# Stores of the S5 tables on ScalarE and GpSimd, sums of squares in four column groups, another order of loads at the second FFN product

## The chip, the cores and the metric

The kernel runs on one core of a Trainium2 chip. Time is device time of one execution in microseconds; lower is better. The five engines have their own instruction streams and work in order: TensorE (PE), VectorE (DVE, `V` in the code), ScalarE (ACT, `S`), GpSimd (POOL, `G`) and SyncE (`SP`), which issues most DMAs. DMAs are issued from SP's, ACT's or POOL's stream and run beside the engines.

## The reference, cut

One inference step of a decoder trunk with two layers, on 1,024 prompt tokens and 64 sample tokens (NT = 1,088), width 1,024, in fp32. Layer 0 mixes tokens by retention and by dilated windowed attention, layer 1 by an S5 state-space model. Behind each mixer stands an FFN, and a norm stands ahead of each.

```python
def rms_norm(x, g):
    xf = x.astype(jnp.float32)
    y = xf * lax.rsqrt(jnp.mean(xf * xf, axis=-1, keepdims=True) + EPS)
    return (y * g.astype(jnp.float32)).astype(x.dtype)

def swiglu(h, w_in, w_out):
    gate, up = jnp.split(h @ w_in, 2, axis=-1)
    return (jax.nn.silu(gate) * up) @ w_out
...
# layer 0:  x += ab_mixer(rms_norm(x));  x += swiglu(rms_norm(x))
# layer 1:  x += s5_mixer(rms_norm(x));  x += swiglu(rms_norm(x));  y = rms_norm(x)
```

The S5 model has 64 groups of 16 channels with 64 complex states each. Its matrices per group (input, output, powers of the state matrix) follow from the weights alone, so they can be worked out at any time before layer 1.

## The kernel before

Activations lie with the features on the 128 partitions: x is eight tiles x[:, m] of 128 features by 1,088 tokens (1,092 with padding). Each fp32 operand is split into a rounded part (hi) and a rest (lo), and each product is three matmuls: hi by hi, and the two mixed ones. ACT writes the hi part, DVE (or POOL) the lo part: `wh_i`/`wl_i` for weights of the second product (`w_unit`, L810 and L811), `wh_p`/`wl_p` for those of the first (L1389, L1390), `f_hi`/`f_lo`, `a_hi`/`a_lo` and others for activations (`load_a`, L1590 and L1591).

`ffn` runs both FFNs. The **first product** (L1414) works on units of 256 columns, each made of seven products of 24 matmuls; weights of a product are split ahead of it, into four buffers. The results go through `put` into a tile `sg`, and from there to a DRAM tensor `a_d` in two stores (L1560). A store is kept in `pending` and issued during the next unit; the last one is `last_store`. The **second product** (`out_proj`, matmuls at L171) goes four times over the eight output tiles m, each time with a part of the 22 activation tiles f: 0 to 4, 5 to 10, 11 to 15, 16 to 21. In the first pass the m are taken in the order FIRST = 6, 7, 4, 5, 2, 3, 0, 1, later from 0 to 7. The result of one (f, m) is collected in one of two PSUM buffers `big` and added to x[:, m] by DVE (L1604), which frees the buffer. Between the products stands the **handover**: f_lo tiles 0 to 4 are loaded from a_d (L1587) and split, the last a_d store is issued, and x is loaded from `x_d` (L1620), each behind the one before (`behind` holds an instruction back until a given one has been placed).

Beside layer 0's FFN runs a background generator, `s5_prep2`: 32 steps `hd`, 16 beside the first product and 16 beside the second, that work out the S5 matrices. A step loads weights (`loads`, L1127 to L1138), transposes on PE (Cs at L1145, Sx at L1209), combines on POOL and DVE (u, Sx, Ox, Ex), and stores to DRAM: Ox (L1181), Ex (L1201) and So (L1212) to `sc_all`, and every second step, after a small product on PE (L1219), Ex again to `sc_p` (L1228). Ex has one buffer. After the last step eight DMAs (L1297) move `sc_p` into `sc_all`. Beside layer 1's FFN the generator is `caches`: POOL copies 4 MB pieces of the key and value caches to the outputs (L1946).

`s5_start` runs the last pass of layer 0's second product with a hook behind each m. The hook squares x[:, m] into `ssq`, sums squares over the features with matmuls (`sums`, L1674, into the PSUM tile `ss`: row block q holds the sums of every eighth token from q), scales x into `hz` and stores it to `h_d` (`put_h`, L1678 and L1679), and loads tables `tb` from `sc_all` (L1720). `s5_in` then makes `S2` and `O2` from a table on ACT (L1782, L1805) and multiplies U by the norm's factor on POOL (L1780).

The order of each engine's stream is set when the program is recorded: a planner places each instruction of the generators and the main line by modelled times, within the bounds that `behind` sets.

## Time and profile before

| | us |
|---|---|
| median of 3 runs | 2646.37 (2642.95 to 2651.38) |
| the profiled execution | 2653.31 |
| its span | 2651.5 |
| PE busy | 2545.2 |
| DVE, ACT, POOL busy | 1499.9, 908.9, 578.4 |

Places in time: layer 0's first product until about 1241, its second product from 1247 to 1564, the S5 model to about 1690; layer 1's first product ends at 2361. The row of a wait reads: engine and line that waited, what released it, us in total, how often, the longest. A timeline's row is start, length, engine, line, operation, tiles, count, and in brackets the idle time ahead of it. In the chain, "issue" is time for which the profile shows no wait. TensorE's clock has two levels, 1.2 and 2.4 GHz; the granted clock of a window is a share of the upper one.

### The profile page before, as it was taken

What the parts mean: (1) busy time and instruction counts of PE and PEld (TensorE: products, weight loads), DVE (VectorE), ACT (ScalarE), POOL (GpSimd) and SP (SyncE); (2) the same over time, 40 slices, a digit from 0 to 9 for tenths busy, and PEclk for the clock granted to TensorE, in tenths of its full rate; (3) what the DMA queues carried; (4) which work ended last, traced back from release to release, by engine and by line L of the source; (5) the groups of instructions that cost most, each with busy time, mean ns of one, the idle gap of its engine ahead of it and who ended that gap; (6) DMA issues with size and microseconds to landing.
All of it is one profiled execution on the core that took longest, in us unless ns stands there. A gap on an engine that the chain in (4) does not pass through costs nothing. (4 is left out here: it accounts for less than half of the span.)

```text
span 2651.5 us, 48165 instructions
## 1 busy us (share of the span) xinstructions
PE 2545.2 (96%) x18861; PEld 2429.4 (92%) x18861; DVE 1499.9 (57%) x3113; ACT 908.9 (34%) x1738; POOL 578.4 (22%) x1117
## 2 busy tenths in 40 slices
PE   8999999999999999999999888999999999999998
PEld 7998788778999999999998877999999999989998
DVE  6223332975677767675666438533766666654335
ACT  5113344665343333232312345422433233222112
POOL 2000021431002677732245424300000000000003
PEclk9999999989999999999999989999999999999999
DMA  8337862214314334353634699411345547478511
GB/s 250 115 96 256 281 230 78 79 35 149 123 54 107 101 106 122 105 136 112 225 107 121 153 246 231 157 58 58 120 161 176 196 172 251 142 273 294 208 66 68
DMA packets 294674, 398.75 MB, mean 150 GB/s; under 512 B 63040, under 2 KB 248288, under 8 KB 293168
## 3 DMA queue, kind: packets, MB, share of 16 engines
q1 hardware_dynamic: 292672, 326.69, 39.9%
q0 software_dynamic: 1776, 68.98, 7.5%
q8 instruction: 150, 2.46, 0.4%
q14 instruction: 76, 0.62, 0.1%
HBM read 303.52 MB, written 163.11 MB: 176 GB/s over the span
## 5 line engine op out<-in xcount | busy, mean ns | idle before, releaser
L1414 PE MATMUL pp<-S_hi,wh_p 128*128 128x272 f32 x1280 | 266.9, 290 | 2.6 <-DVE u L971 2.6
L1414 PE MATMUL pp<-S_hi,wl_p 128*128 128x272 f32 x1280 | 264.1, 287 | 0.0
L1414 PE MATMUL pp<-S_lo,wh_p 128*128 128x272 f32 x1280 | 263.8, 287 | 0.0
L1389 ACT ACTIVATE wh_p<-raw 128x512 fp32r<-128x512 f32 x240 | 149.6, 628 | 289.7 <-PE pp L1414 267.0
L1390 DVE TENSOR_TENSOR wl_p<-raw,wh_p 128x512 fp32r<-128x512 f32 x240 | 182.3, 761 | 101.1 <-ACT wh_p L1389 100.9
L1414 PEld LDWEIGHTS pp<-S_hi,wh_p 128*128 128x128 f32 x1280 | 199.8, 188 | 3.4 <-issue 3.2
L1414 PE MATMUL pp<-A_hi,wh_p 128*128 128x272 f32 x960 | 201.4, 291 | 1.1 <-DVE cs L1431 0.7
L1414 PEld LDWEIGHTS pp<-S_hi,wl_p 128*128 128x128 f32 x1280 | 201.8, 188 | 0.0
L1414 PE MATMUL pp<-A_hi,wl_p 128*128 128x272 f32 x960 | 198.5, 288 | 2.3 <-DVE wl_p L1390 2.3
L1414 PEld LDWEIGHTS pp<-S_lo,wh_p 128*128 128x128 f32 x1280 | 199.9, 188 | 0.0
L1414 PE MATMUL pp<-A_lo,wh_p 128*128 128x272 f32 x960 | 198.6, 288 | 0.0
L1604 DVE TENSOR_TENSOR x<-big,x 128x1092 f32<-128x1092 f32 x64 | 82.7, 1293 | 178.7 <-PE big L171 175.0
L810 ACT ACTIVATE wh_i<-raw 128x1024 fp32r<-128x1024 f32 (+3 forms) x95 | 82.5, 870 | 290.8 <-PE big L171 261.8
L1414 PEld LDWEIGHTS pp<-A_hi,wl_p 128*128 128x128 f32 x960 | 151.4, 188 | 2.8 <-DVE wl_p L1390 2.8
L1414 PEld LDWEIGHTS pp<-A_hi,wh_p 128*128 128x128 f32 x960 | 149.7, 188 | 3.3 <-issue 2.1
L1414 PEld LDWEIGHTS pp<-A_lo,wh_p 128*128 128x128 f32 x960 | 150.1, 188 | 0.1
L811 DVE TENSOR_TENSOR wl_i<-raw,wh_i 128x1024 fp32r<-128x1024 f32 (+3 forms) x93 | 92.3, 993 | 85.7 <-ACT wh_i L810 85.5
L310 PE MATMUL ch<-h_hi,wh_a 128*128 128x364 f32 (+1 forms) x384 | 129.3, 337 | 0.4 <-ACT wh_a L123 0.4
L310 PE MATMUL ch<-h_lo,wh_a 128*128 128x364 f32 (+1 forms) x384 | 128.8, 335 | 0.0
L310 PE MATMUL ch<-h_hi,wl_a 128*128 128x364 f32 (+1 forms) x384 | 128.4, 335 | 0.0
L171 PE MATMUL big<-f_hi,wh_i 128*128 128x364 f32 (+1 forms) x480 | 110.3, 338 | 13.8 <-ACT f_hi L1590 7.7
L171 PE MATMUL big<-f_hi,wl_i 128*128 128x364 f32 (+1 forms) x480 | 108.3, 334 | 0.0
(645 smaller groups left out, 6344.3 us busy)
## 6 DMA issues: line engine op xcount, KB each, us to landing
raw<-in_w_ffn_in SPq DMA_DIRECT2D x44, 1024.0 KB
out_swa_k_sample<-in_state_swa_k POOLq DMA_DIRECT2D x8, 4080.0 KB, 15.9
out_swa_v_sample<-in_state_swa_v POOLq DMA_DIRECT2D x8, 4080.0 KB, 16.0
a_d<-sg SPq DMA_DIRECT2D x44, 544.0 KB
kv<-in_state_swa_k SPq DMA_DIRECT2D x40, 512.0 KB
kv<-in_state_swa_v SPq DMA_DIRECT2D x40, 512.0 KB
x<-x_d SPq DMA_DIRECT2D x24, 546.0 KB
raw<-in_w_in_ab SPq DMA_DIRECT2D x24, 512.0 KB
```

What stands on the lines that cost most here:

```text
L171: last = PE.matmul(pc[c][:, :n], lhsT=w(k), rhs=a(k, c)[:, :n], start=j == 0, stop=j == K * 3 - 1)
L310: PE.matmul(pb[:, :n], lhsT=w[:, k], rhs=a[:, k, c * CH:c * CH + n], start=j == 0, stop=j == 23)
L810: S.activation(hi[:, :n], r, AF.Copy)
L811: split_ins[0] = (eng or V).tensor_tensor(lo[:, :n], r, f32(hi[:, :n]), op=OP.subtract)
L1389: S.activation(hi, src, AF.Copy)
L1390: V.tensor_tensor(lo, src, f32(hi), op=OP.subtract)
L1414: PE.matmul(ps[:, c, :QC], lhsT=w[:, k], rhs=a[:, k, c * QC:(c + 1) * QC], start=n == 0, stop=n == 11)
L1604: V.tensor_tensor(c3(x[:, m]), pb[:, :, :CH], c3(x[:, m]), op=OP.add)
```

## The change

Five edits. Small preparation loads stand behind the x loads in the second half (`box[1]` is the last x load). The stores of Ox and of `sc_p` are issued by POOL, those of Ex, So and hz by ACT. The last a_d store, in both layers, is POOL's, and the x loads go in the order 6, 7, 5, 4, 2, 3, 0, 1 with nothing between them and f_lo. The weight split for the second m of the first pass stands behind the last f_hi. The sums of squares use 32 output rows in four column groups, the squares of m = 6 are added to ssq by VectorE, and two blocks of sums are left, both at m = 7.

```diff
-            SP.dma_start(d16, I["ssm_d"][0].rearrange("(g p) -> p g", p=16), allow_slow_non_contiguous=True)
+            with behind(box[1]):
+                SP.dma_start(d16, I["ssm_d"][0].rearrange("(g p) -> p g", p=16), allow_slow_non_contiguous=True)
...
         def loads(hd):
+            with behind(box[1]):
+                loads_(hd)
+
+        def loads_(hd):
...
-            SP.dma_start(sc_all[:, gs, 128:256], Ox[:, :, 16:])
+            G.dma_start(sc_all[:, gs, 128:256], Ox[:, :, 16:])
...
-            SP.dma_start(sc_all[:, gs, 256:514], Ex)
+            S.dma_start(sc_all[:, gs, 256:514], Ex)
...
-            SP.dma_start(sc_all[:, gs, 0:128], So)
+            S.dma_start(sc_all[:, gs, 0:128], So)
...
-            SP.dma_start(sc_p[:, gs, 112:], Px)
+            G.dma_start(sc_p[:, gs, 112:], Px)
...
-        box, part = [eh], [False]
+        box, part = [eh, None], [False]
...
-            pending.append(lambda sg=sg, gi=gi: [SP.dma_start(a_d[:, gi * 2 + j], sg[:, j]) for j in range(2)][-1])
+            pending.append(lambda q=SP, sg=sg, gi=gi: [q.dma_start(a_d[:, gi * 2 + j], sg[:, j]) for j in range(2)][-1])
...
-            S.activation(hi, lo, AF.Copy)
+            last_hi[0] = S.activation(hi, lo, AF.Copy)
...
-                wv = w_unit(raw, m % 2, n=f1 - f0)
+                with behind(first_hi if m == FIRST[1] and not f0 else None):
+                    wv = w_unit(raw, m % 2, n=f1 - f0)
...
-        with behind(sp[0]):
-            sp[0] = last_store()
+        first_hi = last_hi[0]
+        last_store(G)
         x = x_tile(xr)
-        for m in FIRST:
+        for m in (6, 7, 5, 4, 2, 3, 0, 1):
             with behind(sp[0]):
                 sp[0] = SP.dma_start(x[:, m], x_d[:, m])
+        box[1] = sp[0]
...
             for q in range(8):
-                PE.matmul(ss, lhsT=sel[:, 112 - 16 * q:240 - 16 * q], rhs=perm(t)[:, q], start=first and q == 0, stop=last and q == 7)
+                o = 112 - q % 2 * 16
+                PE.matmul(ss[q // 2 * 32:q // 2 * 32 + 32], lhsT=sel[:, o:o + 32], rhs=perm(t)[:, q], start=first and q % 2 == 0, stop=last and q % 2 == 1)
...
-            SP.dma_start(h_d[m], hs)
+            S.dma_start(h_d[m], hs)
...
                 if m == 6:
+                    V.tensor_tensor(ssq[:, :T], ssq[:, :T], sq, op=OP.add)
+                else:
                     sums(ssq[:, :NT], True, False)
-                sums(sq[:, :NT], False, m == 7)
+                    sums(sq[:, :NT], False, True)
```

SP's stream at layer 0's handover, before (Cs, tE, tA, tF and B are preparation loads; x_15245, x_15246, x_15243, x_15244 are the tiles of m = 6, 7, 4, 5):

```order
L1138 DMA Cs<-in_ssm_c_re 32x64
L1165 DMA tE<-sc_e 128x100
L1181 DMA sc_all<-Ox 128x2x128
L1127 DMA tA<-sc_a 128x108
L1129 DMA tF<-sc_f 128x4
L1133 DMA B_15664<-in_ssm_b_re 64x2x16
L1620 DMA x_15245<-x_d 128x1092
L1620 DMA x_15246<-x_d 128x1092
L1620 DMA x_15243<-x_d 128x1092
L1620 DMA x_15244<-x_d 128x1092
```

The same place after:

```order
L1542 DMA raw<-in_w_ffn_out 128x5x256 x2
L1170 DMA tE<-sc_e 128x100 x2
L1594 DMA f_lo<-a_d 128x1088 x5
L1170 DMA tE<-sc_e 128x100
L1628 DMA x_15245<-x_d 128x1092
L1628 DMA x_15246<-x_d 128x1092
L1628 DMA x_15244<-x_d 128x1092
L1628 DMA x_15243<-x_d 128x1092
```

Between f_lo and x stands one tE load, where a_d stores and two groups of preparation loads stood.

PE's stream around the sums in the last pass, before (the first block on ssq; two more follow, one inside the same product and one behind it):

```order
L171 MATMUL big<-wl_o,wh_i 128x364 x2
L171 MATMUL big<-wl_o,wh_i 128x360
L1674 MATMUL sm<-ssq,t_17986 128x136 x8
L171 MATMUL big<-a_hi,wh_i 128x364 x3
L171 MATMUL big<-a_hi,wl_i 128x364 x2
L171 MATMUL big<-a_hi,wl_i 128x360
```

After, behind the product of m = 7:

```order
L171 MATMUL big<-wl_o,wh_i 128x364 x2
L171 MATMUL big<-wl_o,wh_i 128x360
L1684 MATMUL sm<-ssq,t_17986 32x136 x8
L1684 MATMUL sm<-z_lo,t_17986 32x136 x8
L1802 MATMUL gx<-U,tb 128x136
```

No sums are left between the products; both blocks stand directly ahead of the first S5 product gx.

POOL's stream at layer 1's handover, after (before, neither a_d store stood in it):

```order
L1565 DMA a_d<-sg 128x1088
L1595 MEMSET f_lo 128x4 x2
L1595 MEMSET a_lo 128x4
L1595 MEMSET a 128x4
L1595 MEMSET wl_o 128x4
L1595 MEMSET f_lo 128x4 x3
L1956 COPY s5c<-sg 128x1
L1958 DMA out_swa_v_sample<-in_state_swa_v 64x16320
L1565 DMA a_d<-sg 128x1088
```

One half of the last store stands ahead of a 4 MB copy, the other right behind it.

## Rows read from the trace of the kernel before

**Rows 1.** Page, busy time of each engine over the span.

```profile
PE 2545.2 (96%) x18861; PEld 2429.4 (92%) x18861; DVE 1499.9 (57%) x3113; ACT 908.9 (34%) x1738; POOL 578.4 (22%) x1117
```

**Rows 2.** Busy us (records) of PE, PEld, DVE, ACT, POOL; clock; DMA share; GB/s.

```profile
700.00:1240.00 540.00, 534.22 (x4243) 525.61 (x4242) 382.78 (x659) 181.63 (x363) 233.17 (x482) 1.00 0.36 104
```

**Rows 3.** Waits, 1190 to 1280 us: engine line, releaser: us, times, longest.

```profile
POOL io L1115 <- PE pp L1414: 71.3, 1, 71.3
...
PE big L171 <- ACT f_hi L1590: 5.9, 1, 5.9
...
PE big L171 <- DVE x L1604: 2.0, 1, 2.0
```

**Rows 4.** Waits, 1280 to 1545 us.

```profile
PE big L171 <- ACT wh_i L810: 5.8, 2, 4.4
PE sm L1145 <- ACT So L1211: 5.4, 2, 4.0
...
ACT a_hi L1590 <- DMA a_lo<-a_d: 4.4, 2, 4.2
```

**Rows 5.** Waits, 2340 to 2400 us, handover of layer 1.

```profile
PE big L171 <- DVE x L1604: 4.2, 1, 4.2
```

**Rows 6.** Chain that ended last, 1395 to 1580 us: start us, us, what.

```profile
1486.52 9.81 issue
...
1497.89 1.60 DMA sc_p<-Ex
...
1513.90 10.84 DMA tb<-sc_all
...
1526.53 20.81 PE big L171 x108
1547.34 3.95 PE sm L1674 x16
...
1555.26 3.94 PE sm L1674 x16
```

**Rows 7.** Windows of 7 and 4 us, columns as in rows 2.

```profile
1525.00:1532.00 7.00, 5.47 (x18) 5.28 (x19) 2.93 (x3) 6.31 (x7) 2.54 (x1) 0.52 1.07 369
2382.00:2386.00 4.00, 3.86 (x14) 3.89 (x15) 1.30 (x1) 0.00 (x0) 0.00 (x0) 0.57 1.02 419
```

**Rows 8.** Timeline after m=7: start us, us, engine, line, operation, count [idle before].

```profile
1564.21 1.29 DVE L1604 TENSOR_TENSOR x<-big,x 128x1092 f32<-128x1092 f32 x1 [15.54 <-PE big L171]
...
1566.77 4.33 PE L1674 MATMUL sm<-z_lo,t 128*128 128x136 f32 x16 [2.59 <-ACT z_lo L1690]
```

**Rows 9.** Line 1674, the sums: ns min/median/max, first and last start.

```profile
L1674 PE MATMUL sm<-z_lo,t x32: 403/426/598, 1555.1 to 1570.7; 128*128 128x136 f32 x32
```

**Rows 10.** Timeline of PE in the first product, eight 16-row matmuls.

```profile
901.13 0.41 PE L1219 MATMUL sm<-Ox,Bp 128*16 128x128 f32 x8
```

**Rows 11.** Timeline of SP's queue, handover of layer 0.

```profile
1242.26 2.68 SPq L1587 DMA_DIRECT2D f_lo<-a_d  x5
...
1261.44 4.25 SPq L1620 DMA_DIRECT2D x<-x_d  x8
```

**Rows 12.** Line 1094, a store issued by POOL: ns min/median/max.

```profile
L1094 POOL DMA_DIRECT2D sc_f<-q x1: 570/570/570, 710.3 to 710.3; - x1
```

**Rows 13.** Line 1201, stores of Ex: who waited (us, times).

```profile
  ACT Ex L1199: 78.7, 14
```

**Rows 14.** Timeline of SP's queue, handover of layer 1.

```profile
2363.19 5.96 SPq L1620 DMA_DIRECT2D x<-x_d  x8
2380.74 0.32 SPq L1587 DMA_DIRECT2D a_lo<-a_d  x1
```

**Rows 15.** Timeline of POOL, handover of layer 1.

```profile
2363.51 0.50 POOL L1946 DMA_DIRECT2D out_swa_v_sample<-in_state_swa_v  x1
```

**Rows 16.** Page, DMA issues: count, KB each, us to landing.

```profile
out_swa_v_sample<-in_state_swa_v POOLq DMA_DIRECT2D x8, 4080.0 KB, 16.0
```

More of the change, by code (lines that the diff above doesn't have):

```diff
@@ L1576, in ffn @@
         acts, outs = {}, {}
+        last_hi = [None]
         def load_a(f, slot):
```

## The prediction

> **What bounds the kernel now.** First the page's busy times: TensorE (PE) works in 2545.2 of 2651.5 us, no other engine in more than 57% [rows 1]. So the time can fall only by PE work that goes away or by stretches in which PE stands still, and the next thing to read is where PE stands. In the first product of layer 0's FFN it does not: 534.2 of 540 us are busy at a granted clock of 1.00 [rows 2]. Then the waits of PE in the stretches that the change touches. At the handover from the first to the second product PE waits 5.9 us for the first split of f_lo and later 2.0 us for an addition to x [rows 3]; inside the second product 4.0 us for a small transpose and 4.4 us for a weight split [rows 4]; at layer 1's handover 4.2 us for an addition to x [rows 5]. Last the chain that ended last, between 1480 and 1580 us: it runs through the last stores of the S5 tables, the reads of them, and then through PE, with two of the three sums of squares in it [rows 6]. A standstill of about 4 us is dearer than its length. Behind the 4.4 us the granted clock is 0.52 for 7 us, which is the 1.2 GHz level, and behind the 4.2 us it is 0.57 over 4 us [rows 7]: 7 x 0.48 = 3.4 us and 4 x 0.43 = 1.7 us of PE's work, paid in addition.
>
> All sums are made against the profiled execution, 2653.3 us (span 2651.5). The median of the runs is 2646.4, 6.9 us lower, and I subtract that at the end.
>
> **The sums of squares.** Before, three blocks of eight matmuls with 128 output rows: for ssq inside m=7's product, for m=6 inside it too, and for m=7 behind it. They take 3.95, 3.94 and 4.33 us [rows 6, 8], 16 records each (a matmul of fp32 leaves two), so 0.247 us a record; one record lasts 0.43 us [rows 9], the next starts under it. After, ssq and the square of m=6 are added by VectorE first, and both blocks left stand behind m=7's product, with 32 output rows in four column groups. So 3.95 + 3.94 = 7.9 us leave PE's stream ahead of the end of m=7. The addition costs VectorE about the 1.29 us of an addition to x [rows 8]; it is due only when m=7's product is over, 54 matmuls later, and the sums are all that waits for it. Behind m=7, PE stands 2.59 us until the last square is there [rows 8]; the block on ssq goes into that hole. What remains on the path is the block on m=7's square, 4.33 us before. Its price depends on whether matmuls in different column groups run beside each other. The nearest row is the table product of line 1219, four matmuls of 16 output rows in four groups, where eight of its records take 0.41 us in all [rows 10], less than one record of the sums. If that holds at 136 columns, 16 records take 16/4 x 0.247 = 1.0 us. I take 1.1, since rows 10 show the same arrangement, and gain 3.2. If nothing overlaps, both blocks cost 3.95: the one on ssq sticks out of the hole by 1.4, the other gains 0.4. Together 7.9 + 3.2 = **11.1 us** (6.9 to 11.2).
>
> The Trainium skill ("TensorEngine Tiling (Array Packing)", Key Properties) says that different tiles can execute matmuls in parallel, with which rows 10 agree, and that a change of the tiling mode drains the engine, which speaks against short blocks like these. No row shows a price for that; by it the saving would shrink by two drains.
>
> **Handover of layer 0.** Before, SP issues small loads of S5 preparation, then the five f_lo loads at 1242.3, and the x loads only from 1261.4, behind the last a_d stores and more preparation [rows 11]. After, the preparation loads stand behind the x and a_lo loads, the last store is POOL's, and x follows f_lo at once. The f_lo loads still wait, behind one tE load whose buffer VectorE frees near the product's end, so they start perhaps 1 us sooner, on an emptier queue: I take **1 us** of the 5.9 (-2 to +3, since VectorE now has table work between the last additions and the first subtraction). x of m=6 is there some 10 us before its addition: **2.0 us** go (0 to 2). The order 6, 7, 5, 4 puts first what doesn't wait for the last store. The new w_unit order puts ACT's split for m=7 behind the five f_hi: PE needs it only after 45 matmuls, so it costs nothing.
>
> **Stores on ACT and POOL.** SP loses 32 + 32 + 16 + 32 + 8 stores. The ones of Ox and of sc_p, 48, are POOL's now, about 0.57 us each [rows 12], 27 us of POOL, which is busy in 233 of 540 us [rows 2] and then waits 71 us for the first product to end, since the preparation's first half is done by then [rows 3]; beside PE, nothing. The ones of Ex, So and hz go to ACT, which is busy in 182 of 540. What is queued behind them there are weight splits, and an Ex store waits for VectorE's last operation on Ex. But ACT already waits for these buffers, 78.7 us in 14 waits [rows 13], with PE at 99% beside it, because splits run about three products of 24 matmuls ahead, 9 us. I take **0** for the first product (5 lost to 2 won).
>
> In the second product the 4.0 us wait comes from ACT standing at a_hi for a late a_lo load, with So behind it [rows 4]. SP had issued that load behind a preparation load and an Ox store; the store is gone, the load that waits for POOL is not. I take **1 us** of it (8 won with its clock, 5 lost).
>
> **The S5 tables.** The 4.4 us at 1522 stand for the tables: ACT copies O2 from tb ahead of the split of m=5, and tb lands at 1524.7 [rows 6]. After, these copies stand ahead of the splits of m=6 and m=7. That is one product of 54 matmuls, about 9 us, later; but the last table product on PE also stands 51 matmuls later, so the chain behind it (9.8 us until the copies, the sc_p store, the eight reads, tb [rows 6]) could end later as well. It depends on Ex, buffer by buffer, more than on that product, and its stores no longer wait in SP's row. I expect most of 4.4 + 3.4 to go: **6 us** (0 to 7.8).
>
> **Handover of layer 1.** No preparation runs here, yet x of m=6 is late: its load is issued at 2363.19, behind the last a_d store, 0.3 us ahead of a 4 MB copy that POOL issues at 2363.51 [rows 14, 15], and the next load that needs its lane goes out at 2380.74 [rows 14]. After, that load waits for an addition of the last product, some 2 us earlier, and has the queue to itself; 4.2 + 1.7 = 5.9, I take **5.5** (0 to 5.9). The second half of the last store is now queued behind the copy on POOL's queue, and the load of x for m=4 waits for it, until about 2384: the copy takes 16.0 us [rows 16], and the store comes after it. m=4's addition is due when the fifth product starts, about 2391: four products of 45 matmuls at 0.161 us, which is the 20.81 us of 108 less the 3.4 of clock [rows 6, 7]. SP's later loads wait with it, and the first of them, weights for m=0 and 1, is due at about 2406.
>
> Sum: 11.1 + 1 + 2 + 0 + 1 + 6 + 5.5 = **26.6 us**. 2653.3 - 26.6 = 2626.7 for an execution like the profiled one, 2620 for the median.
>
> **Rivals.** (1) *The tables' chain only moves.* PE comes to m=6 about 4 us sooner, tb lands no sooner, and the wait stands there instead; the preparation's transposes wait more too, since its second half must now fit behind the x loads. For it: the last table product stands 51 matmuls later. Against: 54 matmuls more of cover. The 1 + 6 us are lost, and 5 with them: 26.6 - 12 = 14.6, time 2632. The Trainium skill ("Trainium Kernel Development and Optimization", Key Constraints) holds that DMAs of SP, ACT and POOL run on the same 16 engines and that issuing from several saves issue time alone; this is that rule in this kernel. (2) *The column groups do not overlap* with these strided reads: 4.2 less, 2624. (3) *Layer 1 waits for x of m=4 instead.* If the store lands over 6 us later than I think, the fifth product waits, and behind 4 us its clock goes too: 5.9 lost, 2626 or worse. (4) *Slower.* An Ex store at ACT waits for VectorE and POOL while the next weight split waits behind it. Up to 9 us PE doesn't see it. From there on each us is PE's, and a standstill of 4 us costs 3.4 in clock. If half of the 16 units of the first product go over by 4 us, 8 x 7.4 = 59 us are lost against 26.6 won: 2679. For it: ACT takes its work in order and Ex alternates between two engines. Against: SP held the same stores before, with PE at 99%. (5) *The change doesn't do what it says* in the handover: f_lo no sooner, x late again: 3 less.
>
> **How the numbers follow.** Forecast as summed, with (2), (3) or (5) as small additions: 0.70, between 2608 (all upper ends, 38 won) and 2632. Rival 1: 0.20, 2626 to 2642. Rival 4: 0.06; something else that takes the gain back, near no change: 0.04. The range leaves out rival 4 and the far ends: 2608 to 2640. The bound of 0.3%, about what a measurement of this kernel can tell from no change, is 8 us, so 2638.4. Faster: 0.70 and most of rival 1, 0.84; within: 0.09; slower: 0.07.
>
> **What would show it.** Sums: two blocks of 16 records at line 1684 behind m=7, 1 to 1.5 us each; 4 us each would be rival 2. In the waits, PE's 2.0 for x at 1265 and 4.2 at 2378 gone; 5.9 shortened to about 5. No PE wait on wh_i beside tb near 1520, or one shifted to m=6 (rival 1). In the first product PE busy in 99% still; less is rival 4. What would make it wrong most easily is a new wait of 4 us or more in the second product, for each brings its clock.

## The result, and the profile after

The changed kernel takes 2663.5 us (median; 2657.9 to 2667.8), the kernel before 2646.9 us beside it: a ratio of 1.0055, with an interval of 1.0037 to 1.0072. It is **slower by 0.55%, 14.6 us**. The forecast was 26 us faster, and its range ended at 2640.

The profiled execution of after took 2657.9 us (span 2656.1). It is the quickest of its kernel, while that of before was above its median, so the two traces lie only 4.6 us apart. The trace tells where the time went; how much a part costs is taken from the ratios below. The stretch ahead of layer 0's first product, 790 to 801 us in the traces, has the same work in all kernels and is left out of the table. The table is counted from PE's records; n is the number of the matmul in layer 0's second product. The columns from e1 on are experiments told below.

| us | before | after | e1 | e6 | e7 | e8 | e10 | e11 | e17 |
|---|---|---|---|---|---|---|---|---|---|
| first product, layer 0 | 444.0 | 451.5 | 443.6 | 446.7 | 454.0 | 444.3 | 443.8 | 443.2 | 443.0 |
| handover and n to 90 | 25.5 | 25.2 | 24.6 | 26.6 | 26.3 | 23.9 | 27.6 | 26.7 | 26.0 |
| n 90 to 1152 | 203.2 | 203.2 | 204.6 | 197.3 | 204.9 | 212.3 | 193.2 | 192.0 | 197.6 |
| n 1152 to 1422 | 56.3 | 54.0 | 57.7 | 57.3 | 53.5 | 57.0 | 62.7 | 63.4 | 63.4 |
| n 1422 to 1583 (the end) | 37.4 | 35.8 | 28.6 | 36.4 | 47.5 | 36.7 | 28.9 | 29.1 | 28.9 |
| to the first S5 products | 10.8 | 16.4 | 13.4 | 10.7 | 10.8 | 10.7 | 10.3 | 10.3 | 10.2 |
| S5 model, GLU | 362.5 | 360.6 | 364.7 | 361.4 | 363.3 | 359.9 | 360.4 | 360.7 | 360.4 |
| handover of layer 1, n to 90 | 21.4 | 22.1 | 21.5 | 22.9 | 20.3 | 21.5 | 28.0 | 20.2 | 17.1 |

Layer 1's other stretches agree within 2 us (in e17, whose cache copy is moved, one is 1.6 longer).

The page of after, busy time of each engine, and a window over layer 0's first product (columns as in rows 2):

```profile
PE 2534.4 (95%) x18845; PEld 2419.6 (91%) x18845; DVE 1506.0 (57%) x3114; ACT 909.9 (34%) x1738; POOL 609.9 (23%) x1169
```

```profile
797.00:1240.00 443.00, 435.08 (x3443) 427.87 (x3442) 303.17 (x517) 142.49 (x303) 246.31 (x489) 0.99 0.37 107
```

POOL works 31 us more than in rows 1, in 52 more records: its new stores, 48 of the tables and four of a_d, are counted as its work. In the first product PE is busy in 98.2%, and the same window of before has 98.9%:

```profile
797.00:1241.00 444.00, 439.18 (x3500) 432.12 (x3499) 316.27 (x525) 142.61 (x304) 232.76 (x481) 1.00 0.39 108
```

The waits of PE in after, in order of time, from the first product, the handover, the end of the second product (two rows) and layer 1's handover:

```profile
PE sm L1150 <- ACT So L1216: 4.4, 2, 3.1
...
PE big L171 <- ACT f_hi L1597: 8.1, 1, 8.1
...
PE big L171 <- ACT wh_i L810: 6.6, 1, 6.6
...
PE gx L1802 <- POOL U L1792: 12.4, 1, 12.4
...
PE big L171 <- DVE x L1612: 3.0, 1, 3.0
```

The first row has no counterpart in before. The wait for f_hi was 5.9 [rows 3], that for wh_i 4.4 and one product earlier [rows 4], that for x in layer 1 4.2 [rows 5]. The sums themselves came out as forecast (timeline of PE):

```profile
1564.11 1.20 PE L1684 MATMUL sm<-ssq,t 128*32 128x136 f32 x16
1566.77 1.20 PE L1684 MATMUL sm<-z_lo,t 128*32 128x136 f32 x16 [1.47 <-ACT z_lo L1700]
1580.34 0.82 PE L1802 MATMUL gx<-U,tb 128*128 128x136 f32 x2 [12.37 <-POOL U L1792]
```

Two blocks of 16 records, 1.2 us each instead of 3.95 and 4.33 [rows 6, 8], and behind them 12.4 us of nothing.

### The profile page after: what moved, and what is told of

It is laid out like the page before. It is cut to its first block, busy times and chain, and to the rows that moved or that the text cites. A ratio compares the mean times of both kernels' runs of the same rounds, so it can differ in the third digit from the quotient of the medians.

```text
span 2656.1 us, 48079 instructions
## 1 busy us (share of the span) xinstructions
PE 2534.4 (95%) x18845; PEld 2419.6 (91%) x18845; DVE 1506.0 (57%) x3114; ACT 909.9 (34%) x1738; POOL 609.9 (23%) x1169
## 4 chain that ended last, share of the span: by engine, by line
PE 44%; DMA 6%; DVE 4%; POOL 3%; issue 2%; ACT 1%; SPq 1%; ACTq 0%; DVEq 0%; POOLq 0%
PE pp L1419 21%; PE big L171 17%; PE big L940 2%; PE pp L940 2%; DMA sc_all<-Ex 1%; DMA U<-h_d 1%; PE pb L1992 1%; POOL u L1160 1%; DMA tb<-sc_all 1%; DVE Ex L1201 1%; DVE Ex L1203 1%; DMA tE<-sc_e 1%; DVE v L1202 0%; DMA sc_all<-sc_p 0%; POOL Ex L1201 0%
## 5 line engine op out<-in xcount | busy, mean ns | idle before, releaser
L1395 DVE TENSOR_TENSOR wl_p<-raw,wh_p 128x512 fp32r<-128x512 f32 x240 | 175.6, 733 | 115.8 <-ACT wh_p L1394 115.8
L171 PE MATMUL big<-f_hi,wh_i 128*128 128x364 f32 (+1 forms) x480 | 110.0, 338 | 12.4 <-ACT f_hi L1597 9.1
L171 PE MATMUL big<-f_lo,wh_i 128*128 128x364 f32 (+1 forms) x480 | 108.9, 335 | 1.1 <-DVE f_lo L1598 1.1
```

Source lines behind the costliest of these rows:

```text
L171: last = PE.matmul(pc[c][:, :n], lhsT=w(k), rhs=a(k, c)[:, :n], start=j == 0, stop=j == K * 3 - 1)
L1395: V.tensor_tensor(lo, src, f32(hi), op=OP.subtract)
```

## The experiments

All ratios are to the kernel before on the same chip, with their intervals. 1.001 is 2.65 us.

**The parts of the change, one at a time (e1 to e4).** e1 is before with the hunks of `sums` and `hook` alone. e2 has the stores alone, e3 the handover alone, e4 the whole change without the held preparation loads. The four edits in this order, cut to their core:

```diff
-                PE.matmul(ss, lhsT=sel[:, 112 - 16 * q:240 - 16 * q], rhs=perm(t)[:, q], start=first and q == 0, stop=last and q == 7)
+                PE.matmul(ss[q // 2 * 32:q // 2 * 32 + 32], lhsT=sel[:, o:o + 32], rhs=perm(t)[:, q], start=first and q % 2 == 0, stop=last and q % 2 == 1)
```

```diff
-            SP.dma_start(sc_all[:, gs, 128:256], Ox[:, :, 16:])
+            G.dma_start(sc_all[:, gs, 128:256], Ox[:, :, 16:])
...
-            SP.dma_start(h_d[m], hs)
+            S.dma_start(h_d[m], hs)
```

```diff
+            with behind(box[1]):
...
-            sp[0] = last_store()
+        last_store(G)
...
-        for m in FIRST:
+        for m in (6, 7, 5, 4, 2, 3, 0, 1):
...
+                with behind(first_hi if m == FIRST[1] and not f0 else None):
```

```diff
-            with behind(box[1]):
-                loads_(hd)
+            loads_(hd)
```

> The kernel before with the edit of the sums alone (32 output rows in four column groups, ssq and the square of m=6 added by VectorE). Theory: this part did what was forecast, since the changed kernel's trace shows two blocks of about 1.1 and 1.2 us behind m=7. About 11 us faster than before, 2636. Rival: PE standing in the last pass waits for the S5 tables anyway, so that PE comes sooner to the same wait: 0 to 4 us faster, with a longer wait on wh_i beside tb or at gx.

> The kernel before with the stores of Ox and sc_p on POOL, and of Ex, So and hz on ACT, nothing else. Theory A (ACT holds weight splits while an Ex store waits for POOL or VectorE): the first product of layer 0 takes about 451 us instead of 444, the row of wh_p released by Ex in the waits of 800 to 1240 us is there with some 30 us, and the time is 5 to 8 us above before, 2653. Theory B (all of the loss is from the loads that stand behind x): the first product stays at 444 us, the time is that of before or some us lower, 2643 to 2647.

> The kernel before with the loads at the second product alone: preparation loads behind x, the last store on POOL, the order 6, 7, 5, 4 and the split behind f_hi; all other stores on SP as before, sums as before. Theory B: POOL waits some 34 us for preparation loads after 1245, the last sc_p store leaves 15 us or more after the 1497.9 of before, gx starts 8 to 12 us later relative to the second product's start; 8 to 15 us slower than before, 2658. Theory A: the handover itself gains, the x wait of 2.0 us and part of layer 1's 4.2 are gone; 3 to 6 us faster, 2642.

> The changed kernel with the preparation loads where they stood before (not behind x); everything else of the change is in. Theory B: the tables' chain ends as before or sooner, gx follows the sums without 12 us of waiting; 20 us or more below the changed kernel, 2637 to 2642. Theory A: the first product still takes 451 us, and the time is within 10 us of the changed kernel's 2663.

Measured: e1 0.9991 (0.998 to 1.0002), e2 1.0051 (1.0032 to 1.0069), e3 1.0044 (1.0028 to 1.0061), e4 1.0058 (1.0044 to 1.0073). So the sums bring nothing measurable (the rival of that expectation), the stores cost 13.5 us alone and the handover 12 (theory A of the stores and theory B of the handover, the first dearer than expected), and e4 is no faster than the change (theory A). These do not add up to 14.6, and they need not: each version has its own order of the streams. e3 and e4 lose 5 to 7 us at layer 1's handover in a way that the change does not; e18 below shows why.

In e1 the 8.8 us of the sums are there (37.4 to 28.6) and most of them are given back in three places of the table: 1.4 ahead of them, 2.6 at the first S5 products, 2.2 behind. The second is ACT's. Its timeline in e1 around the end of the second product:

```profile
1555.72 2.00 ACT L810 ACTIVATE wh_i<-raw 128x1024 fp32r<-128x1024 f32 x2 [3.08 <-DMA raw<-in_w_glu]
...
1568.45 4.39 ACT L1679 ACTIVATE hz<-x,g_mix 128x1088 f32<-128x1088 f32 x2 [3.98 <-DMA h_d<-hz]
```

The splits of the first GLU weights stand ahead of the square root (L139) of the norm's factor. Before, PE came so late that their load was there. Now ACT waits 3.1 for it and splits for 2.0, and the root starts 5.1 later than its input is ready.

**Moving that split (e5).** The sums, and the split behind the root:

```diff
-            with tc.issue_after(s5["sq"].ins) if m == 0 else ExitStack():
+            with tc.issue_after(sq_ins[0].ins) if m == 0 else ExitStack():
```

> The kernel before with the edit of the sums, and the first two GLU weight splits placed on ACT behind the square root of the norm's factor instead of behind the last square. Theory A, the gain of the sums is eaten by ACT standing at a late GLU load ahead of that root: the root starts about 5 us sooner than with the sums alone (3.1 of waiting and 2.0 of splitting), PE's wait for U at the first S5 product falls from 9.4 to 4 to 5 us, and the time is 4 to 6 us below that of the sums alone, about 0.997 of the kernel before. Theory B, what bounds the start of the S5 model is the DMA queue (loads of U and tables): the root is sooner, PE only waits at the next product, and the time stays at 0.999.

Measured: 0.9993 (0.9979 to 1.0008), theory B. PE reaches the first S5 product 5.6 us sooner (13.4 to 7.8) and then stands at the second (waits of PE, and ACT's timeline in e5):

```profile
PE gx L1794 <- ACT S L1786: 10.6, 2, 9.5
```

```profile
1580.66 4.38 ACT L1679 ACTIVATE hz<-x,g_mix 128x1088 f32<-128x1088 f32 x2 [7.54 <-DMA h_d<-hz]
```

ACT waits for a hz buffer, whose store stands in SP's row behind a series of table loads; the last four stores of hz go out only from 1575.16. That is 72.5 us behind the last sc_p store, as in e1; in before it is 76.1. So SP's row came 3.6 us sooner with the sums, and no sooner with e5's edit. That this row bounds the stretch is argued from these times and not shown, since no run shortens it alone; e11 below, which takes the hz stores out of it, ends within the noise of e6.

**Which stores (e6, e7).** e6 has the stores of Ex and So on ACT, e7 those of Ox and sc_p on POOL:

```diff
-            SP.dma_start(sc_all[:, gs, 256:514], Ex)
+            S.dma_start(sc_all[:, gs, 256:514], Ex)
...
-            SP.dma_start(sc_all[:, gs, 0:128], So)
+            S.dma_start(sc_all[:, gs, 0:128], So)
```

```diff
-            SP.dma_start(sc_all[:, gs, 128:256], Ox[:, :, 16:])
+            G.dma_start(sc_all[:, gs, 128:256], Ox[:, :, 16:])
...
-            SP.dma_start(sc_p[:, gs, 112:], Px)
+            G.dma_start(sc_p[:, gs, 112:], Px)
```

> The kernel before with the stores of Ex and So alone issued by ACT. Theory A, a store of Ex on ACT waits for POOL's part of Ex and holds the copy So behind it, for which PE waits: the first product of layer 0 takes 451 to 452 us instead of 444, waits of PE at the transposes on ACT's So appear, and the time is 8 to 13 us above the kernel before (1.003 to 1.005). Theory B, the stores of hz on ACT or those on POOL cost it: first product 444 us, time within 3 us of before.

> The kernel before with the stores of Ox and of sc_p alone issued by POOL. Theory A, these cost nothing as forecast, since POOL has idle time and nobody waits for it: time within 3 us of before. Theory B, a store of sc_p on POOL waits for its data and holds the combinations of the next step: first product longer by some us, time 4 to 8 us above before.

Measured: e6 0.9969 (0.9954 to 0.9984), **8 us faster**, and e7 1.0052 (1.0032 to 1.0073), 14 us slower. Both went against my theory A: from the trace of after I had blamed the Ex store on ACT. ACT stands there in the first product with a weight split behind the store, in after (first row) and, for less long, in e6 (second row):

```profile
ACT wh_p L1394 <- POOL Ex L1203: 34.1, 6, 9.1
```

```profile
ACT wh_p L1389 <- POOL Ex L1198: 22.1, 5, 5.7
```

Yet e6 is the faster kernel, so the store by itself is not the cause; POOL being late is. In e7 the first product takes 454.0 with no store on ACT at all. In e2, which has both edits and the hz stores, the 8 us of e6 are not there (13.5 beside the 14 of e7); whether a late POOL turns ACT's stores from a gain into a loss was not separated. SP's row loses 64 stores in e6, and the second product between n = 90 and 1152 is 5.9 shorter; where else the 8 us come from, one trace does not tell.

Why POOL cannot carry 48 stores is not plain from its busy time. Before, POOL is busy in 27.9, 42.3, 33.6, 33.8, 42.6 and 35.1 us of the six windows of 50 us from 850 to 1150, the preparation's first half; the two fullest (columns as in rows 2, POOL is the fifth pair):

```profile
900.00:950.00 50.00, 50.00 (x404) 48.67 (x403) 34.46 (x48) 15.75 (x38) 42.30 (x94) 1.00 0.36 100
...
1050.00:1100.00 50.00, 49.91 (x402) 48.39 (x401) 33.24 (x49) 16.00 (x38) 42.62 (x86) 1.00 0.36 105
```

85% there and 72% over the six, where the share that the prediction read is 233 of 540 us [rows 2]. The stores' own rows in e7 (line views: ns min/median/max), and a piece of POOL's timeline:

```profile
L1181 POOL DMA_DIRECT2D sc_all<-Ox x32: 739/748/764, 855.1 to 1504.2; - x32
```

```profile
L1228 POOL DMA_DIRECT2D sc_p<-Ex x16: 532/560/565, 898.8 to 1520.5; - x16
```

```profile
1055.26 1.14 POOL L1158 TENSOR_TENSOR Ox<-u,u 128x288 f32<-128x288 f32 x1
1056.68 0.74 POOL L1181 DMA_DIRECT2D sc_all<-Ox  x1 [0.29 <-POOL Ox L1158]
...
1060.82 0.56 POOL L1228 DMA_DIRECT2D sc_p<-Ex  x1 [0.29 <-POOL Ex L1227]
```

13 of the 32 and 14 of the 16 also wait 0.29 for POOL's own result, so the stores take 24 + 9 + 8 = 41 us over both products, about half of it in the first. POOL is idle for 85 of the 300 us there, so the time would fit. What counts is what stands behind the stores, in the waits of e7 from 1055 to 1073 us:

```profile
ACT Ex L1199 <- POOL u L1155: 6.7, 1, 6.7
...
PE pp L1414 <- DVE cs L1431: 3.1, 1, 3.1
DVE wl_p L1390 <- ACT wh_p L1389: 2.8, 1, 2.8
```

Read from the top: ACT's copy into the one Ex buffer starts at 1063.74, when the sc_p store above lands (POOL's u, which is named, ends in the same moment; e14 below names the store); behind it stands a weight split wh_p; DVE waits for that split with the additions that empty PE's buffers behind it; PE stands 3.1. Later the same lateness puts the last sc_p store at 1520.5, and PE waits 11.2 us for a weight split in the last pass.

**Ox or sc_p (e13, e14).** Each of the two alone:

```diff
-            SP.dma_start(sc_all[:, gs, 128:256], Ox[:, :, 16:])
+            G.dma_start(sc_all[:, gs, 128:256], Ox[:, :, 16:])
```

```diff
-            SP.dma_start(sc_p[:, gs, 112:], Px)
+            G.dma_start(sc_p[:, gs, 112:], Px)
```

> The kernel before with the 32 stores of Ox alone issued by POOL. Theory A, each store takes 0.75 us of POOL and 0.3 us of waiting ahead of it, in a stretch in which POOL has no idle time that it could use: this is most of the 16 us, 9 to 13 us over before, first product 450 us or more. Theory B, the stores of sc_p are the cost, since Ex's one buffer waits for them: this run is within 4 us of before.

> The kernel before with the 16 stores of sc_p alone issued by POOL. Theory A, POOL's time counts: 16 times 0.85 us, a third of that of Ox, 3 to 5 us over before. Theory B, the store stands in POOL's row behind the next step's operations, Ex comes free later, and ACT holds the weight splits: 10 to 16 us over before.

Measured: e13 1.0001 (0.9989 to 1.0013), e14 1.0014 (1.0002 to 1.0027), together 1.0052. e13 comes out as its theory B and e14 as its theory A, so neither part is the cost by itself. The 29 us of the Ox stores, with their waits, fit into POOL's idle time alone. The sc_p stores cost 4 us, and e14's waits of ACT (1050 to 1075) and PE (the first product) show the chain of e7:

```profile
ACT Ex L1199 <- DMA sc_p<-Ex: 6.0, 1, 6.0
```

```profile
PE pp L1414 <- ACT wh_p L1389: 3.4, 2, 3.2
```

The sum of the parts is 4, and both together cost 14. That the Ox stores use up the slack in which this chain would else run unseen is the likely reason; no run shows the slack itself.

**The held loads (e8).** Before, with the loads of the preparation behind the x loads:

```diff
+            with behind(box[1]):
+                loads_(hd)
...
+        box[1] = sp[0]
```

> The kernel before with the loads of the S5 preparation alone held behind the x loads; last store, order of x and of splits as before. Theory A, the handover's loss is that of the held loads: the second half of the preparation starts late, its last store ends 10 us or more later, PE waits for the splits behind tb's copies and for the start of the S5 model, and the time is 5 to 12 us above before. Theory B, the loss is in the last store on POOL and in the x loads of layer 1: time within 3 us of before here.

Measured: 1.0028 (1.0012 to 1.0044), theory A, 7 us. Waits at the handover and, second row, until 1450:

```profile
POOL Bp L1175 <- DMA B<-in_ssm_b_im: 43.0, 2, 40.3
...
PE sm L1150 <- ACT So L1216: 9.0, 3, 4.7
```

POOL, which paces the preparation, stands 40 us for its first loads. In before it stands in this stretch too, for 10.3 and 33.2 us, but with one step's combinations done; the last sc_p store of e8 is at 1500.8 instead of 1497.9, behind a first product that ended 4.3 sooner, so it is 7 later. The x addition is on time (25.5 to 23.9 at the handover), and n 90 to 1152 takes 9.1 us more.

**Undoing parts of the change (e9, e10), and the sums with ACT's stores (e11, e12).** e9 is the change with this edit, and e10 is e9 with the edit of e4 in addition:

```diff
-            G.dma_start(sc_all[:, gs, 128:256], Ox[:, :, 16:])
+            SP.dma_start(sc_all[:, gs, 128:256], Ox[:, :, 16:])
...
-            G.dma_start(sc_p[:, gs, 112:], Px)
+            SP.dma_start(sc_p[:, gs, 112:], Px)
```

e11 is e1 with this and e6's edit, e12 is e11 with the edit of e5:

```diff
-            SP.dma_start(h_d[m], hs)
+            S.dma_start(h_d[m], hs)
```

> The changed kernel with one part undone: the stores of Ox and sc_p are SP's again. Theory A, these two stores are what makes the change slow, because POOL has no idle time in the stretch of the preparation (store alone: 16 us over before): the first product of layer 0 takes 445 to 447 us instead of 451.5, and the time is 10 to 15 us below the changed kernel, at 2649 to 2654 beside 2650 of before. Theory B, any store that leaves SP in company with the held loads costs it: first product still 451 to 452, time still 1.004 to 1.006 of before.

> The changed kernel with two parts undone: the stores of Ox and sc_p are SP's, and the preparation loads are not held behind the x loads. Theory A, the held loads cost about the 7 us that they cost alone: time 4 to 8 us below the run with them held, some 0.997 to 0.999 of before. Theory B, without the held loads x comes late at both handovers, as in the changed kernel without holding: no gain, or 2 to 5 us lost, against the run with them held.

> The kernel before with the edit of the sums and the stores of Ex, So and hz on ACT, nothing else. Theory A, the sums' gain was eaten by loads and stores in SP's row between the last sc_p store and the start of the S5 model, among them the second pair of hz stores; with hz on ACT the 4.0 us wait of ACT for the hz buffer goes, and the time is below that of the Ex and So stores alone (0.9969): 0.993 to 0.996, 2632 to 2640. Theory B, the transfers themselves bound the start of the S5 model, whoever issues them: 0.996 to 0.998.

> The run before this one, and the first two GLU weight splits on ACT behind the square root of the norm's factor. Theory A, ACT standing at the GLU load ahead of the root is a cost of its own once hz does not wait in SP's row: 3 to 5 us below the run without this edit. Theory B, the S5 stretch is bound by transfers, and a split placed later is late for the GLU's first product: same time within 2 us, or slower.

Measured: e9 1.0016 (1.0003 to 1.003), e10 1.0011 (1.0002 to 1.002), e11 0.9962 (0.9946 to 0.9978), e12 0.9975 (0.9964 to 0.9985): theory A for e9, theory B for the other three, e11 at the edge of its two ranges. From e11 up to the change this is a ladder:

| | ratio | step, us |
|---|---|---|
| e11: sums, Ex, So and hz on ACT | 0.9962 | -10 from before |
| e10: and last store on POOL, order of x, first_hi | 1.0011 | +13 |
| e9: and the loads held | 1.0016 | +1 |
| the change: and Ox, sc_p on POOL | 1.0055 | +10 |

The 1 us of the third row is not the price of the held loads. In the traces e9 loses 13.9 against e10 between n = 90 and 1152 (207.1) and wins 7.4 at layer 1's handover (20.6), where its order of the streams is another; the next run separates the two. e12 confirms e5: placing the GLU split later brings nothing.

**The last store on POOL (e18).** Of the step of 13 us, 7.8 lie in the traces of e10 and e11 at layer 1's handover. e10 there, SP's timeline and PE's wait:

```profile
2361.50 0.38 SPq L1537 DMA_DIRECT2D raw<-in_w_ffn_out  x1
2361.93 4.40 SPq L1623 DMA_DIRECT2D x<-x_d  x8
```

```profile
PE big L171 <- DVE x L1607: 8.9, 1, 8.9
```

With no store ahead of x in SP's row, the planner placed a weight load there, which waits for its buffer until 2361.5, 18 us behind the 4 MB copy. The same order stands in e3, where PE's wait for x is 9.1 and the table's row would be 26.8:

```profile
2375.80 0.38 SPq L1542 DMA_DIRECT2D raw<-in_w_ffn_out  x1
2376.22 4.79 SPq L1628 DMA_DIRECT2D x<-x_d  x8
```

It stands in e4 too (10.9 and 28.5), but not in after and e9, where x follows f_lo. e18 is e10 with that load behind the first x load, in layer 1:

```diff
-                    load_out(raw, f0, f1, m)
+                    with behind(x6[0] if l and not f0 and m == 0 else None):
+                        load_out(raw, f0, f1, m)
```

> The changed kernel with SP's stores of Ox and sc_p and without the held preparation loads (1.0011 of before), and in layer 1 the third weight load of the second product held behind the first load of x. Theory A, that weight load, which waits in SP's row for a buffer, made x of m=6 late: the first 90 matmuls of layer 1's second product take 20 us or less instead of 27, and the time is 6 to 10 us lower, 0.997 to 0.999. Theory B, the POOL stores around the 4 MB copy make x late in any order: 25 us or more, time as before this edit.

Measured: 0.9983 (0.9967 to 0.9999), theory A; x is next behind f_lo in SP's row, and the stretch with the gap takes 20.6 instead of 28.0:

```profile
2363.65 24.32 SPq L1625 DMA_DIRECT2D x<-x_d  x8
```

```profile
PE big L171 <- DVE x L1609: 3.0, 1, 3.0
```

So the planner's order at this one place is worth 7 us, and some 5 of the 12 us of e3 and 6 of the 15 of e4 are likely its doing: e4 does not show that the held loads cost nothing. e9 and e18 have the same order here and differ in the held loads alone, 1.0016 and 0.9983: these cost 9 us, near the 7 of e8.

3.0 stays, as in after. There x of m=6 is issued 2.5 us ahead of the copy, and the x loads take 25 us to be issued, since that of m=4 waits for the half of the store behind the copy (SP and POOL of after):

```profile
2365.21 24.95 SPq L1628 DMA_DIRECT2D x<-x_d  x8
```

```profile
2367.74 0.50 POOL L1958 DMA_DIRECT2D out_swa_v_sample<-in_state_swa_v  x1
2368.23 0.54 POOL L1565 DMA_DIRECT2D a_d<-sg  x1
```

**Moving the copy, and the wait ahead of the S5 model (e15 to e17).** e15 and e16 are e11 with one edit each, e17 has both and issues the last weight load of the second product ahead of the loads of xs and tb. In e15 `held` is ACT's part of the last weight split, and the copies into fz and O2 stand in the same block:

```diff
+        with tc.issue_after(held.ins) if q < 4 else ExitStack():
+            S.activation(zc[:, :, 128:], x0[:, :, g0:g0 + 2].rearrange("p b g -> p g b"), AF.Copy)
```

```diff
-                for _ in range(7):
+                for _ in range(9 if (b, nm) == (5, "k") else 7):
                     yield
```

```diff
+                if hook and m == 4:
...
+                    s5["raw6"] = load_out(ahead6[0], f0, f1, 6)
...
+            if m == 4:
+                with behind(s5["raw6"]):
+                    SP.dma_start(s5["xs"], sc_x)
+                    for i in range(4):
+                        load_t(i)
```

> The version with the sums and the stores of Ex, So and hz on ACT (0.9962 of before), and the copies into Zc and O2 of the first four S5 steps held on ACT behind the last weight split of the second product. Theory A, ACT stood at these copies for tb with weight splits and an hz store behind it: PE's 10.2 us wait before the product of m=5 goes, with its clock, and the end of the second product comes 10 to 14 us sooner; of that at least 5 are left behind the S5 start: 0.990 to 0.994. Theory B, tables and U come no sooner, so PE waits at the first S5 products instead: 0.995 to 0.997.

> The version with the sums and the stores of Ex, So and hz on ACT (0.9962 of before), and the 4 MB cache copy that POOL issues at layer 1's handover issued two products later, the later ones shifted with it. Theory A, x of m=6 is late because of that copy: PE's 3.0 us wait for the addition to x goes, the first 90 matmuls of layer 1's second product take 15 to 16 us instead of 18.4, time 2 to 4 us lower. Theory B, x is late because its loads are issued behind the last stores: the wait stays at 2 us or more and the time within 2 us.

> The sums, the stores of Ex, So and hz on ACT, the cache copy two products later, the copies into Zc and O2 held behind the last weight split, and the load of the weights for m = 6 and 7 of the last pass issued ahead of the loads of xs and tb. Theory A, the wait ahead of the S5 start is the order in SP's row: PE's wait of 10 us behind m=5 falls to 3 us or less, and of it and its clock at least 5 us are left in the time: 0.991 to 0.994 of before. Theory B, the tables' transfers bound the start of the S5 model: the wait turns up at the first S5 products, whose wait for U or tb grows from 6 to 12 us or more, and the time is 0.995 to 0.997.

Measured: e15 0.9967 (0.9953 to 0.9981), e16 0.9958 (0.9943 to 0.9972), e17 0.9949 (0.9932 to 0.9967). e16: PE's wait for x is gone (18.4 to 15.3 from the first matmul to n = 90), so the copy was its cause, but in this trace the next stretch, up to n = 360, is 3.6 longer than in e11, and the ratio doesn't tell it from e11. e15 and e17 did not touch the 10.2 us that PE stands ahead of m = 5 in the last pass, so neither of their theories holds, and they show why. ACT's timeline in e15:

```profile
1522.20 0.33 ACTq L1680 DMA_DIRECT2D h_d<-hz  x1
1522.58 0.84 ACT L810 ACTIVATE wh_i<-raw 128x768 fp32r<-128x768 f32 x1 [21.81 <-DMA raw<-in_w_ffn_out]
```

and in e17:

```profile
1505.95 2.50 ACT L1684 ACTIVATE hz<-x,g_mix 128x1088 f32<-128x1088 f32 x1 [0.27 <-DMA h_d<-hz]
1530.13 0.33 ACTq L1685 DMA_DIRECT2D h_d<-hz  x1
1530.50 0.84 ACT L810 ACTIVATE wh_i<-raw 128x768 fp32r<-128x768 f32 x1 [22.05 <-DMA tb<-sc_all]
```

The last row reads as if the split waited for a table, which it never uses. What waits is the **store of hz, issued by ACT, ahead of it**: its data is there at 1508.5, and it goes out at 1530.1. In the compiled program the store waits on two semaphores: for its scaling, and on a counter of DMA completions that the stores of ACT share with the loads of SP. Its turn on that counter comes after a load of tb in e17, after the last weight load in e11 and e15 (the split reads weights that an earlier load brought), and so PE's weights wait for a transfer that has nothing to do with them. In after a store of hz stands in the same way:

```profile
1527.69 2.51 ACT L1688 ACTIVATE hz<-x,g_mix 128x1088 f32<-128x1088 f32 x1 [0.72 <-DMA h_d<-hz]
1541.08 0.33 ACTq L1689 DMA_DIRECT2D h_d<-hz  x1
1541.66 0.47 ACT L1814 ACTIVATE Zc<-xs 128x16 f32<-128x16 f32 x3 [11.46 <-DMA tb<-sc_all]
...
1543.00 0.84 ACT L810 ACTIVATE wh_i<-raw 128x768 fp32r<-128x768 f32 x1
```

hz is ready at 1530.2, its store goes out at 1541.1, the split at 1543.0: PE's 6.6. But here the load that the store waits for is the very table that the copies into O, between the store and the split, read. Without the store ACT would have stood for it at these copies, so in after the 6.6 us are the late table's. The cost in the other versions shows in the table: n 1152 to 1422 takes 57 us in e1 and e6, which leave hz on SP, and 63 in e10, e11 and e17, which don't. The version that follows, e17 with the stores of hz on SP, was not tried: that the stop goes with the store, and what this would bring, is open.

## Why the prediction was wrong, point by point

**The stores on POOL, priced at 0, cost 10 to 14 us.** This is the step that failed first: e7 has them alone (14), e9 undoes them (10). It took POOL's busy time over 540 us for room, where the preparation's first half has 72%, and two of its windows 85%. "Beside PE, nothing" was wrong above all in kind: POOL paces Ex, Ex paces ACT, and ACT's splits pace PE. e7 and e14 show that chain, e13 shows that the time of the Ox stores alone does no harm. Rival 4 had the sign, the place and ACT's row, and named an edit that alone is 8 us faster (e6, forecast at 0 and 1). It had 0.06.

**The sums, 11.1 us, were right as a saving and wrong as a gain.** 1.2 us a block (1.1 forecast), 8.8 of the stretch saved in e1, and 2.4 of the time, which the interval does not tell from nothing. The prediction asked what hides an edit's cost, and not what hides its gain. In e1 that is ACT's weight split first, and behind it, as e5 suggests and does not prove, SP's row of table, U and GLU loads. The Trainium skill ("TensorEngine Tiling (Array Packing)", Key Properties) says that a change of the tiling mode drains the engine. At 1.2 us a block the trace leaves no such price to be seen. In after the root's wait behind the GLU split is 8.1 us, and 12.4 stand where 11.1 were saved.

**The S5 tables, 6 us.** Rival 1 came true, place and reason: the wait moved to m=6, 6.6 instead of 4.4, because the chain ends later. The last sc_p store is at 1515.1 instead of 1497.9 [rows 6], 13 us later behind the first product's end, with POOL late and the loads held. In e10, e11 and e17, where the chain is not that late, the store of hz on ACT brings a stop of 10.2 to 10.5 us in its place; the prediction had that store in a term of 1 and saw no wait for it.

**The handover of layer 0, 3 us.** The 2.0 for x went as forecast. f_lo did not come sooner, but later, at 1246.78 where before had 1242.26 [rows 11]. SP, POOL and ACT at the handover of after:

```profile
1236.73 10.00 SPq L1170 DMA_DIRECT2D tE<-sc_e  x2
1246.78 3.46 SPq L1594 DMA_DIRECT2D f_lo<-a_d  x5
```

```profile
1246.09 0.57 POOL L1565 DMA_DIRECT2D a_d<-sg  x1 [9.43 <-DVE Ex L1203]
```

```profile
1246.74 0.41 ACTq L1206 DMA_DIRECT2D sc_all<-Ex  x1
...
1252.71 1.11 ACT L1597 ACTIVATE f_hi<-f_lo 128x1092 fp32r<-128x1092 f32 x1 [0.83 <-DMA f_lo<-a_d]
```

PE's work ahead of the handover ends at 1241.7 in before and 1245.7 in after, so f_lo is issued 0.6 and 1.1 behind it: 0.5 later where 1 sooner was forecast, since VectorE frees the tE buffer that late. And the first f_lo is 5.9 on its way (1246.8 to 1252.7), against 4.1 before: POOL issues a half of the last store 0.7 ahead of it, which stood behind the f_lo loads on SP before, and ACT a store of Ex in the same moment; which of them slows it was not separated. Together 2.3, just past the lower end of the term, and they cancel the 2.0. The held loads, which had no price at all, cost 7 alone and 9 beside the rest (e9 against e18).

**The handover of layer 1, 5.5 us.** x of m=6 was issued 2.5 ahead of the copy, and PE's wait for it is still 3.0; 1.2 us of the wait went, and the stretch is 0.7 longer all the same. e16 shows what the step missed: in after not the queue ahead of x was in the way, but the copy beside it.

One sum of the prediction is off without touching the result: the upper ends of all its terms add up to 39.9, and the 38 won behind its 2608 leave out the 2 won in the first product.

The Trainium skill ("DMA: Bandwidth & Descriptors", Issuing engines are not separate DMA queues) says that issuing from several engines saves only the time to initiate a DMA. In e6, where SP's row is 64 stores shorter, the time is 8 us lower; e7 and e17 show the other side, that the issuing engine pays with its own row, 0.75 us for a store of Ox on POOL and 22 us once on ACT.

## What to carry to other kernels

Price a store moved to another engine by that engine's busiest stretch and by what stands behind the store in its row, and follow everything that it may wait for, its completion counter included. Price a saving on PE by what is second in the same stretch: here 8.8 us saved on PE left 2.4, within the noise. When several edits touch one engine with little slack, measure them together too: 0 and 4 us alone were 14 together. And compare two versions with the order of their streams beside them: one weight load ahead of x, placed by the planner, was 7 us.

The fastest version measured is e17, at 0.9949 of before: sums and ACT's stores, SP's handover, a cache copy moved by two products, the copies into O2 held and one weight load ahead. Its interval overlaps those of e11, e15 and e16.

## What the runs showed that I had not expected

Sixteen records at 32 rows in four column groups took 1.20 us, against 3.95 at 128 rows, with the change of shape inside it. A DMA issued by ACT held that engine for 22 us, though its data was ready, because it counts its completion where SP's loads do; the profile's row names a tile that neither the store nor the instruction behind it reads. A 546 KB load of x issued 2.5 us ahead of a 4 MB copy cost PE as much as one issued 0.3 ahead of it, 3.0 us in both e18 and e11. And the planner's place for one weight load was worth 7 us, half of what the whole change cost.
